# A hybrid attention layer: how the projections of the next head pair are dealt among the attention blocks of the current one

## The chip, the cores and the metric

The kernel runs on one core of a Trainium2 chip. The metric is the device time of one execution in microseconds. Three runs of the kernel before took 1989.61, 1990.07 and 1990.54 us (median 1990.07). The profile is of one more execution, which took 1991.46 us and whose profiled span is 1989.6 us.

## The reference, cut to what matters

The reference is one encoder layer, applied to two sequences with the same weights: a prompt of 1024 tokens (R below) and a sample of 512 tokens (S). Width 1024, heads of 64.

```python
hn = rms_norm(x, g_attn)
qa, ka, va, qd, kd, vd = split(hn @ w_in, 6)          # 8 heads each
oa = neighbourhood_attention(qa, ka, va, rpb)          # 2-D window, learned bias
od = dilated_attention(qd, kd, vd, slopes)             # three dilated windows merged
x  = x + concat(rms_norm(oa), rms_norm(od)) @ w_out
x  = x + (silu(hn2 @ w_gate) * (hn2 @ w_up)) @ w_down  # hn2 = rms_norm(x)
y  = rms_norm(x)
```

All of it is float32. The kernel multiplies float32 numbers as a sum of three products of high and low parts, so every projection of 128 features by 512 tokens is 8 x 3 = 24 matmuls. Probabilities and values are multiplied as float16 high and low parts.

## The kernel before, in words

The work up to about 850 us is projections and attention. Heads are taken two at a time ("pairs"): 16 pairs, first eight of R, then eight of S, alternately of kind b (dilated, heads `qd kd vd`) and kind a (neighbourhood). They are numbered from 0 here, as in the code: 0, 2, 4, 6 are R b; 1, 3, 5, 7 are R a; 8, 10, 12, 14 are S b; 9, 11, 13, 15 are S a.

A pair needs its projections: values, queries and keys, in this order (`ORDER`), each for every chunk of 512 tokens (two in R, one in S). That is 144 matmuls for an R pair and 72 for an S pair, all of line 155 (`mm3`, tile `acc`). A chunk's result is read out of its PSUM bank by `v_put`, `q_put` or `k_put`: ACT makes copies (high parts), DVE subtracts them from the bank (low parts). There are two such banks.

Then the pair's attention runs in blocks of 128 queries, 16 blocks in an R pair and 8 in an S pair: all blocks of its first head (`k.i` is 0), then all of its second (`k.i` is 1). `k.j` counts the blocks within a head, `k.st.nq` is their number. A block is on PE the scores (tile `sc`, lines 701 and 702), on DVE their sum with a bias table and the row's minimum (line 742), on ACT the exponentials (tile `t`, line 752), on PE the transposes of those (tile `pt`, line 763), on ACT the high part (line 769) and on DVE the low part (line 773) of the transposed, and for two blocks at a time on PE the product with the values (tile `pv`, line 785).

`step` writes the blocks out as a software pipeline. One step has the transposes of the block before, the softmax of this one, the value product of an earlier two, the scores of the next one, and then projections of a later pair from a generator, `dense`: `advance` draws one portion and `spent` counts the portions; `target` says how many portions are to be spent after a block. A portion is six matmuls, so an R pair's projections are 24 portions, an S pair's 12 (`totals`). `LEAD` shifts the target by so many blocks. Before the first scores of a new pair, `step` draws portions until that pair's keys are marked complete (`whole`).

Work that must come some portions later is put on an `agenda` by `after(n, ...)`; every portion drawn calls `tick`, which counts down. A chunk is read out two portions after its last matmul; low parts follow one portion later.

In most pairs PE, ACT and DVE execute in the order in which this code writes instructions (`manual_schedule`, the variable `core`). The exceptions are the blocks during which the projections of pair 4, of pair 7 and of pair 15, and after them the first output tiles, are dealt (`loose`): there a scheduling layer of the program orders the engines. These are, up to a few blocks at either end, the attention blocks of pairs 3, 6, 14 and 15.

Of the kernel before, what the change touches and what calls it, by code (L numbers as in the profile page):

```python
# [31 lines left out]
EPS = 1e-6  # L32
BW = 1600
LAG = 3
LEAD = 2
SQ = 4
TL = 3
NO = 4
# [18 lines left out]
def hymba_layer_kernel(  # L57
# [92 lines left out]
    def mm3(out, ops, first=True):  # L150

        i, last = 0, 3 * len(ops) - 1
        for (ah, al, bh, bl) in ops:
            for a, b in ((ah, bh), (ah, bl), (al, bh)):
                latest[0] = nc.tensor.matmul(out=out, lhsT=a, rhs=b, start=first and i == 0, stop=i == last,  # L155
                                              skip_group_check=not first)
                i += 1
                if i % 6 == 0:
                    yield

    agenda = []

    def after(n, fn):
        agenda.append([n, fn])

    def tick():
        for e in list(agenda):
            e[0] -= 1
            if e[0] <= 0:
                agenda.remove(e)  # L170
                e[1]()
# [3 lines left out]
            agenda.pop(0)[1]()  # L175

    def run(gen):
        for _ in gen:
            tick()

    order = [("b", 0), ("a", 0), ("b", 1), ("a", 1), ("b", 2), ("a", 2), ("b", 3), ("a", 3)]
    pairs = [(st, g, c) for st in (R, S) for g, c in order]
# [188 lines left out]
    def qkv(pi):  # L371
# [7 lines left out]
        def proj(which, ch):  # L379
            u = base + ORDER.index(which)  # L380
            w_split(u)
            wh, wl = ready[u]
            if u + 1 < n_in:
                w_load(u + 1)
            hh, hl = hT[st.name, ch]
            if which == 0:
                hh, hl = (z.rearrange("p k (q n c) -> p k n q c", q=8, n=4) for z in (hh, hl))
            acc = bank("tp" if pi == 0 and which == 1 else "mm", "acc")
            for i, _ in enumerate(mm3(acc, [(wh[:, k, :], wl[:, k, :], hh[:, k], hl[:, k]) for k in range(NK)])):
                if i == 1 and ch == st.nch - 1:  # L390
                    if u + 1 < n_in:
                        w_split(u + 1)
                    if u + 2 < n_in:
                        w_load(u + 2)
                if i == 3:
                    if pi:
                        after(2, lambda: (q_put, k_put, v_put)[which](ch, acc))
                    else:
                        (q_put, k_put, v_put)[which](ch, acc)
                yield  # L400

        def dst(z, ch):
            if g == "a":
# [92 lines left out]
        def k_put(ch, acc):  # L496
            if ch == 0:
                if st is S:
                    z = rb.tile([P, 2, T], F32R, tag="ka", name="ka", bufs=3)
                    res["k"] = [z[:, i] for i in range(2)]  # L500
                else:
                    res["k"] = [rb.tile([P, nx], F32R, tag="ka", name=f"ka{i}", bufs=3) for i in range(2)]
                res["kl"] = [klow[i][:, :nx] for i in (0, 1 + pi % 2)]
            ka, kl = res["k"], res["kl"]
            for n in range(2):
                for i in range(2):
                    nc.scalar.activation(dst(ka[i], ch)[own[i - n]], rev(acc[own[i]]), AF.Copy)

            def low(i):
                nc.vector.tensor_tensor(out=dst(kl[i], ch)[own[i]], in0=rev(acc[own[i]]),  # L510
                                        in1=dst(ka[i], ch)[own[i]].bitcast(F32), op=ALU.subtract)
                if ch == st.nch - 1 and nx > T:
                    borders(ka[i])
                    borders(kl[i], own[i])

            def lows():
                low(0)
                low(1)
                if ch == st.nch - 1:
                    res["whole"] = True  # L520

            after(1 if pi else 2, lows)

# [22 lines left out]

        done[pi] = res
        if pi == 0:
            rest = opening(proj)
            for _ in rest:  # L550
                yield
            return
# [13 lines left out]
        if by_chunk:  # L566
            turns.sort(key=lambda z: z[1])
        for which, ch in turns:
            for _ in proj(which, ch):
                next(extra, None)  # L570
                yield
        for _ in extra:
            yield

# [315 lines left out]
        yield  # L890

    def out_tile(i, ahead):
        for j, _ in enumerate(out_mm(i, st_out["wo"])):
            if j == 0:
                out_norm(i + 1)
            if j == 2 and i + 2 < ahead:
                out_pre(i + 2)
            if j == 5:
                out_tr(i + 1)
            yield  # L900

    def out_first():
        yield from out_start()
# [10 lines left out]
    def stream():  # L914
        for pi in range(1, len(pairs)):
            at[0] = pi
            for _ in qkv(pi):
                yield
        at[0] = len(pairs)
        yield from out_first()  # L920

# [2 lines left out]

    def advance(n=1):
        for _ in range(n):
            if next(dense, "end") == "end":
                return
            tick()
            spent[0] += 1  # L930

    def target(pi, j):

# [11 lines left out]
    def step(g):  # L945
# [20 lines left out]
            scores(todo[g + 1])  # L966
        if g + TL < len(todo):
            tables(todo[g + TL])
        while spent[0] < target(k.pi, k.j):
            was = spent[0]  # L970
            advance()
            if spent[0] == was:
                break
# [11 lines left out]
    while g < len(todo):  # L985
        with ExitStack() as fixed:
# [3 lines left out]
            while g < len(todo) and (at[0] in loose) == now:  # L990
                step(g)
                g += 1
    for _ in dense:
        tick()
    flush()
    while owed:
        head_out(owed.pop())
# [505 lines left out]
```

## Time and profile before

| | |
|---|---|
| median of 3 runs | 1990.07 us |
| profiled execution, its span | 1991.46 us, 1989.6 us |
| PE busy, share of the span | 1843.8 us, 93% |
| DVE busy | 1320.6 us, 66% |
| ACT busy | 915.6 us, 46% |
| POOL busy | 843.3 us, 42% |
| mean granted clock of TensorE | 0.973 |

The page divides the span in 40 slices of about 50 us; the first 17 or so are projections and attention, the rest the output projection and the feed-forward part. PE is the matmul engine, PEld its weight loads, which run beside matmuls. A matmul's shown duration is longer than the time to the next one's start, since they are pipelined; how fast PE goes is read from starts. Where PE has nothing to do, the timeline shows in brackets how long and what ended it.

The pairs stand in the trace one after the other. In the windows below a pair begins with the first score matmul of its first block and ends with that of the next pair's.

### The profile page before, as it was taken

The page shows a single profiled execution, that of the slowest core. Times are in us where ns is not written, and L with a number is a line of the kernel's source. Part 1 is how long each engine was busy: PE and PEld are TensorE (multiplying, and loading weights), DVE is VectorE, ACT ScalarE, POOL GpSimd, SP SyncE. Part 2 cuts the span into 40 slices and gives each one's busy share as a digit, 9 for nine tenths or more (in the row PEclk, how much of TensorE's full clock was granted, in tenths as well). Part 3 has the DMA queues.
Part 4 walks back from the last instruction along what each step waited for, and adds up shares of the span by engine and source line. Part 5 has one row for each costly group of instructions (what it writes and reads, how often), then busy time and mean ns, then how long its engine had stood idle before and what let it go on. Part 6 is the DMA issues. An engine that isn't in the chain of part 4 may idle for free.

```text
span 1989.6 us, 28959 instructions
## 1 busy us (share of the span) xinstructions
PE 1843.8 (93%) x10450; PEld 1619.5 (81%) x10450; DVE 1320.6 (66%) x2626; ACT 915.6 (46%) x1731; POOL 843.3 (42%) x691
## 2 busy tenths in 40 slices
PE   5899999989889998999899999989999997999998
PEld 4677777777677776878799999989999995887886
DVE  6565657755665556667877877787677764756765
ACT  4364566655566666444433334344333332423431
POOL 3223342233245543200466766766666652652120
PEclk9898999999999999999999999989999998999999
DMA  9333243332344445444334434433434438866652
GB/s 264 110 81 88 65 111 80 78 96 59 84 95 115 114 125 172 134 144 157 106 114 129 141 101 130 116 86 118 131 113 119 120 119 317 276 222 224 216 182 93
DMA packets 218943, 265.97 MB, mean 134 GB/s; under 512 B 59584, under 2 KB 163152, under 8 KB 218800
## 3 DMA queue, kind: packets, MB, share of 16 engines
q1 hardware_dynamic: 196176, 179.57, 29.7%
q0 software_dynamic: 22624, 84.56, 14.4%
q8 instruction: 82, 1.34, 0.3%
q14 instruction: 61, 0.50, 0.1%
HBM read 202.71 MB, written 51.41 MB: 128 GB/s over the span
## 4 chain that ended last, share of the span: by engine, by line
PE 47%; DMA 5%; DVE 4%; issue 3%; POOL 2%; ACT 1%; SPq 0%; DVEq 0%; POOLq 0%; ACTq 0%
PE acc L155 16%; PE yacc L155 13%; PE zacc L155 8%; PE mmacc L155 8%; DMA wq<-in_w_down_dram 2%; DMA left<-hid_d 1%; POOL wq L1284 1%; DVE flo L1126 1%; PE pt L210 1%; DMA hid_d<-as 1%; DMA wo_raw<-in_w_out_dram 0%; DVE left L1301 0%; ACT left L1300 0%; DVE dlo L1274 0%; POOL as L1244 0%
## 5 line engine op out<-in xcount | busy, mean ns | idle before, releaser
L155 PE MATMUL acc<-dhi,left 128*128 128x512 f32 x924 | 290.2, 395 | 15.4 <-ACT left L1300 13.6
L155 PE MATMUL acc<-hth,whi 128*128 128x512 f32 x576 | 236.3, 410 | 10.1 <-ACT hth L290 7.6
L155 PE MATMUL acc<-htl,whi 128*128 128x512 f32 x576 | 233.3, 405 | 6.8 <-POOL htl L293 3.7
L155 PE MATMUL acc<-hth,wlo 128*128 128x512 f32 x576 | 233.0, 405 | 0.9 <-POOL wlo L125 0.6
L1126 DVE TENSOR_TENSOR flo<-fs,fhi 128x512 fp32r<-128x512 f32 x176 | 174.8, 996 | 76.4 <-ACT fhi L1125 72.3
L773 DVE SCALAR_TENSOR_TENSOR pT<-pt,pT 128x512 f16<-128x512 f32 (+2 forms) x256 | 136.8, 553 | 132.5 <-ACT pT L769 130.9
L155 PEld LDWEIGHTS acc<-dhi,left 128*128 128x128 f32 x924 | 174.5, 189 | 56.1 <-ACT left L1300 14.4
L125 POOL TENSOR_TENSOR wlo<-wraw,whi 128x1024 fp32r<-128x1024 f32 x48 | 114.5, 2388 | 197.5 <-ACT whi L124 197.5
L1125 ACT ACTIVATE fhi<-fs 128x512 fp32r<-128x512 f32 x176 | 109.5, 628 | 183.4 <-POOL fs L1130 60.1
L769 ACT ACTIVATE pT<-pt 128x512 f16<-128x512 f32 (+2 forms) x256 | 118.9, 489 | 162.6 <-PE pt L763 159.3
L155 PE MATMUL acc<-dlo,left 128*128 128x512 f32 x462 | 181.8, 394 | 0.0
L1130 POOL TENSOR_TENSOR fs<-fraw 128x512 f32<-128x512 f32 x88 | 130.3, 1497 | 80.0 <-DMA fraw<-in_w_up_dram 70.0
L763 PE MATMUL pt<-ident,t 128*128 128x128 f32 x768 | 122.8, 282 | 44.2 <-ACT t L752 39.7
L1126 DVE TENSOR_TENSOR flo<-fraw,fhi 128x512 fp32r<-128x512 f32 x132 | 162.1, 1228 | 0.6 <-ACT fhi L1125 0.4
L1284 POOL TENSOR_TENSOR wq<-wq 128x512 f32<-128x512 f32 x55 | 93.2, 1706 | 157.9 <-DMA wq<-in_w_down_dram 128.2
L763 PEld LDWEIGHTS pt<-ident,t 128*128 128x128 f32 x768 | 89.8, 143 | 76.6 <-ACT t L752 56.9
L752 ACT ACTIVATE t<-t,mt 128x768 f32<-128x768 f32 (+3 forms) x192 | 137.9, 718 | 25.8 <-DVE mt L742 23.3
L1125 ACT ACTIVATE fhi<-fraw 128x512 fp32r<-128x512 f32 x132 | 83.0, 629 | 122.2 <-PE yacc L155 95.3
L155 PEld LDWEIGHTS acc<-hth,whi 128*128 128x128 f32 x576 | 111.8, 194 | 33.1 <-ACT hth L290 8.7
L155 PEld LDWEIGHTS acc<-htl,whi 128*128 128x128 f32 x576 | 112.1, 195 | 30.1 <-DVE htl L293 4.5
L155 PEld LDWEIGHTS acc<-hth,wlo 128*128 128x128 f32 x576 | 111.6, 194 | 28.7 <-POOL wlo L125 3.6
L1301 DVE TENSOR_TENSOR left<-left,left 128x1408 fp32r<-128x1408 f32 x42 | 74.4, 1774 | 81.6 <-ACT left L1300 81.5
(219 smaller groups left out, 4863.8 us busy)
## 6 DMA issues: line engine op xcount, KB each, us to landing
wq<-in_w_down_dram SPq DMA_DIRECT2D x132, 256.0 KB
hid_d<-as POOLq DMA_DIRECT2D x22, 1344.0 KB, 8.1
left<-hid_d SPq DMA_DIRECT2D x42, 704.0 KB
wraw<-in_w_in_dram POOLq DMA_DIRECT2D x46, 512.0 KB, 4.8
fraw<-in_w_gate_dram SPq DMA_DIRECT2D x45, 512.0 KB
fraw<-in_w_up_dram SPq DMA_DIRECT2D x45, 512.0 KB
tabb<-in_tabb_dram POOLq DMA_DIRECT2D x8, 800.0 KB, 5.6
xh<-x_d SPq DMA_DIRECT2D x12, 512.0 KB
```

The costliest lines, as they stand in the source:

```text
L125: eng.tensor_tensor(out=lo, in0=src, in1=hi.bitcast(F32), op=ALU.subtract))
L155: latest[0] = nc.tensor.matmul(out=out, lhsT=a, rhs=b, start=first and i == 0, stop=i == last, skip_group_check=not first)
L210: nc.tensor.transpose(out=pts[k // 4][:, k % 4 * P:(k % 4 + 1) * P], in_=src[:, k * P:(k + 1) * P], identity=ident)
L752: nc.scalar.activation(k.t, k.t, AF.Exp, bias=k.mt, scale=-1.0, accum_out=k.den)
L763: nc.tensor.transpose(out=pt[:, c * P:(c + 1) * P], in_=k.t[:, (c0 + c) * P:(c0 + c + 1) * P], identity=ident)
L769: nc.scalar.activation(hi, pt, AF.Copy, scale=16384.0)
L773: nc.vector.scalar_tensor_tensor(out=lo, in0=pt, scalar=16384.0, in1=hi, op0=ALU.mult, op1=ALU.subtract)
L1125: nc.scalar.activation(hi, src, AF.Copy)
L1126: nc.vector.tensor_tensor(out=lo, in0=src, in1=hi.bitcast(F32), op=ALU.subtract)
L1130: nc.gpsimd.tensor_tensor(out=o, in0=a, in1=b, op=op)
L1284: nc.gpsimd.tensor_tensor(out=src, in0=src, in1=other, op=q[1])
L1301: nc.vector.tensor_tensor(out=lo, in0=raw_lo, in1=hi.bitcast(F32), op=ALU.subtract)
```

## The change

Four things are changed.

`target` is called with the block's number in the pair, `k.i * k.st.nq + k.j`, where it was called with its number in the head, `k.j`.

`mm3` hands over after three matmuls instead of six. The first of two hand-overs is marked False; it draws no `tick`, and `spent` counts each as half a portion. So the agenda counts in the same six matmuls as before.

`LEAD` is 3 instead of 2.

`k_put` makes the first two of a key chunk's four ACT copies (those that the low parts are subtracted from) when it is called, and the other two one portion later, right before the low parts. The border columns of a b pair's keys in R are copied after both low parts and one portion later, and keys are marked complete one portion later as well.

```diff
-LEAD = 2
+LEAD = 3
...
-                if i % 6 == 0:
-                    yield
+                if i % 3 == 0:
+                    yield i % 6 == 0
...
     def run(gen):
-        for _ in gen:
-            tick()
+        for whole in gen:
+            if whole is not False:
+                tick()
...
-            for i, _ in enumerate(mm3(acc, [(wh[:, k, :], wl[:, k, :], hh[:, k], hl[:, k]) for k in range(NK)])):
+            i = -1
+            for whole in mm3(acc, [(wh[:, k, :], wl[:, k, :], hh[:, k], hl[:, k]) for k in range(NK)]):
+                if not whole:
+                    yield False
+                    continue
+                i += 1
...
-            for n in range(2):
+            def copy(n):
                 for i in range(2):
                     nc.scalar.activation(dst(ka[i], ch)[own[i - n]], rev(acc[own[i]]), AF.Copy)
 
+            copy(0)
+
             def low(i):
                 nc.vector.tensor_tensor(out=dst(kl[i], ch)[own[i]], in0=rev(acc[own[i]]),
                                         in1=dst(ka[i], ch)[own[i]].bitcast(F32), op=ALU.subtract)
-                if ch == st.nch - 1 and nx > T:
-                    borders(ka[i])
-                    borders(kl[i], own[i])
-
             def lows():
-                low(0)
-                low(1)
+                copy(1)
+                for i in range(2):
+                    low(i)
                 if ch == st.nch - 1:
-                    res["whole"] = True
+                    if nx > T:
+                        after(1, lambda: [borders(*z) for i in range(2) for z in ((kl[i], own[i]), (ka[i],))])
+                    after(1, lambda: res.update(whole=True))
...
-            if next(dense, "end") == "end":
+            whole = next(dense, "end")
+            if whole == "end":
                 return
-            tick()
-            spent[0] += 1
+            if whole is not False:
+                tick()
+            spent[0] += 1 if whole is None else 0.5
...
-        while spent[0] < target(k.pi, k.j):
+        while spent[0] < target(k.pi, k.i * k.st.nq + k.j):
```

Counted on PE between the first scores of one block and those of the next, the projection matmuls stand like this (pair 4 is like pairs 1, 2 and 5; pair 8 like 9 to 12):

| pair, its blocks | before | now |
|---|---|---|
| 0 (16) | 60 30 6 12 6 12 6 12 6 0 0 0 0 0 0 66 | 56 36, then 9 in each of 14 |
| 4 (16) | 0 18 6 12 6 12 6 12 6 0 0 0 0 0 0 66 | 9 in each |
| 6 (16, loose) | 12 20 2 16 1 9 0 0 20 3 1 0 24 0 24 12 | 9 9 10 8 9 9 0 0 24 0 51 3 0 0 0 12 |
| 7 (16) | 0 6 0 6 6 6 0 6 6 0 0 0 0 0 0 36 | 0 0, then 6 and 3 in turn in 12, 9 9 |
| 8 (8) | 0 18 6 12 6 0 0 30 | 9 in each |
| 13 (8) | 0 18 6 12 6 0 0 42 | 9 9 9 9 9 9 2 22 |

Pair 2 has 155 before and 148 now, pair 3 (loose) 133 and 140.

PE in the second head of pair 5 (R a), two blocks' scores (`sc`), transposes (`pt`) and the value product after them (`pv`); before:

```order
L701 MATMUL sc_4818<-ka1_4336,qa1_3890 128x384
L702 MATMUL sc_4818<-kl2_94,qa1_3890 128x384
L763 MATMUL pt_4826<-ident_69,t_4799 128x128 x3
L701 MATMUL sc_4839<-ka1_4336,qa1_3890 128x384
L702 MATMUL sc_4839<-kl2_94,qa1_3890 128x384
L763 MATMUL pt_4843<-ident_69,t_4830 128x128 x3
```

PE at the same blocks of pair 5, with a projection (`acc`) of pair 6; now:

```order
L709 MATMUL sc_4864<-ka1_4130,qa1_3860 128x384
L710 MATMUL sc_4864<-kl2_94,qa1_3860 128x384
L155 MATMUL acc_4829<-hth_104,whi_4674 128x512
L155 MATMUL acc_4829<-htl_105,whi_4674 128x512
L155 MATMUL acc_4829<-hth_104,wlo_4675 128x512
L155 MATMUL acc_4829<-hth_104,whi_4674 128x512
L155 MATMUL acc_4829<-htl_105,whi_4674 128x512
L155 MATMUL acc_4829<-hth_104,wlo_4675 128x512
L155 MATMUL acc_4829<-hth_104,whi_4674 128x512
L155 MATMUL acc_4829<-htl_105,whi_4674 128x512
L155 MATMUL acc_4829<-hth_104,wlo_4675 128x512
L771 MATMUL pt_4891<-ident_69,t_4845 128x128 x3
```

Three times the three products of a projection (high by high, low by high, high by low) now stand between a block's scores and the transposes of the block before it, where nothing stood.

DVE at the end of pair 1 (R a), when pair 2's keys become complete: low parts of keys (`kl0`, `kl1`, lines 510 and 518), borders (lines 413, 414, 419 and 420) and the scores' sums (`t,mt`, lines 742 and 750); before:

```order
L510 TENSOR_TENSOR kl0_92<-acc_1953,ka0_1960 64x512
L413 COPY ka0_1960<-ka0_1960 128x128
L414 COPY ka0_1960<-ka0_1960 128x128
L413 COPY kl0_92<-kl0_92 64x128
L414 COPY kl0_92<-kl0_92 64x128
L510 TENSOR_TENSOR kl1_93<-acc_1953,ka1_1961 64x512
L413 COPY ka1_1961<-ka1_1961 128x128
L414 COPY ka1_1961<-ka1_1961 128x128
L413 COPY kl1_93<-kl1_93 64x128
L414 COPY kl1_93<-kl1_93 64x128
L742 ISA t_2030,mt_2031<-sc_2019,tabb_1872 128x512
L742 ISA mt_2031 128x1
```

DVE at the same place; now:

```order
L518 TENSOR_TENSOR kl0_92<-acc_1832,ka0_1839 64x512
L518 TENSOR_TENSOR kl1_93<-acc_1832,ka1_1840 64x512
L419 COPY kl0_92<-kl0_92 64x128
L420 COPY kl0_92<-kl0_92 64x128
L419 COPY ka0_1839<-ka0_1839 128x128
L420 COPY ka0_1839<-ka0_1839 128x128
L419 COPY kl1_93<-kl1_93 64x128
L420 COPY kl1_93<-kl1_93 64x128
L419 COPY ka1_1840<-ka1_1840 128x128
L420 COPY ka1_1840<-ka1_1840 128x128
L750 ISA t_2006,mt_2007<-sc_1977,taba1_99 128x384
L750 ISA mt_2007 128x1
```

Both low parts come first and the borders after them, and a sum over a block of pair 1 (table `taba`) still follows them; before, the next sum was pair 2's first (table `tabb`).

## Rows read from the trace of the kernel before

**Rows 1.** Page, parts 1 and 2: busy time by engine; 40 slices
```profile
PE 1843.8 (93%) x10450; PEld 1619.5 (81%) x10450; DVE 1320.6 (66%) x2626; ACT 915.6 (46%) x1731; POOL 843.3 (42%) x691
...
PE   5899999989889998999899999989999997999998
...
PEclk9898999999999999999999999989999998999999
```

**Rows 2.** Windows by pair: length; busy (x instructions) PE, PEld, DVE, ACT, POOL; PEclk; DMA
```profile
86.40:148.20 61.80, 57.67 (x438) 48.92 (x437) 42.23 (x111) 39.96 (x81) 17.25 (x17) 1.00 0.27 69
148.20:208.50 60.30, 55.77 (x338) 45.61 (x338) 29.28 (x80) 30.34 (x68) 20.30 (x21) 0.92 0.29 79
208.50:282.60 74.10, 68.89 (x515) 58.15 (x514) 50.44 (x138) 45.23 (x92) 24.30 (x25) 1.00 0.31 80
328.70:401.20 72.50, 67.42 (x518) 57.12 (x517) 49.67 (x134) 45.61 (x95) 24.30 (x28) 1.00 0.29 74
401.20:459.00 57.80, 52.83 (x353) 43.04 (x352) 31.62 (x88) 31.90 (x70) 22.61 (x23) 1.00 0.30 82
459.00:531.60 72.60, 67.24 (x422) 53.50 (x421) 49.11 (x127) 41.40 (x80) 21.12 (x23) 0.95 0.30 78
531.60:548.80 17.20, 11.04 (x100) 9.00 (x98) 11.31 (x24) 7.80 (x17) 4.26 (x7) 0.91 0.31 95
548.80:585.10 36.30, 31.24 (x225) 25.00 (x223) 22.02 (x66) 22.94 (x56) 17.03 (x19) 1.00 0.47 103
641.40:671.10 29.70, 27.22 (x175) 21.75 (x174) 16.38 (x42) 18.87 (x39) 15.14 (x14) 1.00 0.45 104
671.10:697.40 26.30, 23.96 (x152) 19.62 (x150) 13.98 (x43) 15.37 (x38) 14.06 (x12) 1.00 0.48 119
727.10:758.80 31.70, 27.44 (x173) 22.15 (x171) 16.42 (x47) 16.07 (x39) 13.79 (x13) 1.00 0.47 127
```

**Rows 3.** Windows of two blocks without projections, and of a slow clock
```profile
115.19:120.37 5.18, 4.16 (x45) 3.63 (x45) 4.52 (x15) 3.57 (x8) 0.75 (x2) 1.00 0.36 119
568.59:572.15 3.56, 2.37 (x22) 1.71 (x22) 2.40 (x8) 2.17 (x6) 2.08 (x3) 1.00 0.35 95
183.80:194.10 10.30, 8.98 (x47) 7.33 (x48) 4.71 (x15) 4.42 (x13) 2.79 (x4) 0.50 0.28 89
```

**Rows 4.** Timeline of PE: one transpose of a block without projections, and its wait
```profile
115.19 0.88 PE L763 MATMUL pt<-ident,t 128*128 128x128 f32 x6 [1.01 <-ACT t L752]
```

**Rows 5.** Windows of two blocks with 18 projection matmuls; last row: four blocks
```profile
353.76:361.85 8.09, 8.09 (x63) 6.93 (x62) 6.68 (x18) 6.57 (x13) 2.07 (x3) 1.00 0.26 52
160.55:166.78 6.23, 6.23 (x41) 5.23 (x40) 3.70 (x11) 2.66 (x7) 1.40 (x2) 1.00 0.46 132
594.02:600.80 6.78, 6.78 (x48) 5.66 (x47) 4.33 (x14) 4.62 (x11) 6.51 (x7) 1.00 0.29 78
623.74:629.29 5.55, 5.55 (x35) 4.60 (x34) 3.21 (x12) 3.39 (x9) 4.50 (x5) 1.00 0.32 72
229.10:245.30 16.20, 15.85 (x123) 13.41 (x121) 13.86 (x37) 10.65 (x22) 5.91 (x6) 1.00 0.32 68
```

**Rows 6.** Timeline of PE: two successive projection matmuls in a long run
```profile
207.82 0.40 PE L155 MATMUL acc<-hth,whi 128*128 128x512 f32 x1
208.05 0.39 PE L155 MATMUL acc<-htl,whi 128*128 128x512 f32 x1
```

**Rows 7.** Waits, 75 to 900 us: total, times, longest
```profile
PE pt L763 <- ACT t L752: 39.7, 53, 1.2
...
PE sc L702 <- DVE kl L510: 3.6, 7, 1.6
...
DVE kl L510 <- ACT ka L507: 64.5, 22, 5.3
```

**Rows 8.** Lines of DVE in the third pair: low part of a key, border copy
```profile
L510 DVE TENSOR_TENSOR kl<-acc,ka 64x512 fp32r<-64x512 f32 x6 | 4.1, 688 | 10.3 <-ACT ka L507 10.2
...
L413 DVE CAST ka<-ka 128x128 fp32r<-128x128 f32 x2 | 0.4, 217 | 0.0
```

More of the change, by code (lines that the diff above doesn't have):

```diff
@@ L399, in proj @@
                         (q_put, k_put, v_put)[which](ch, acc)
-                yield
+                yield True
         def dst(z, ch):
@@ L548, in qkv @@
         if pi == 0:
-            rest = opening(proj)
+            rest = opening(lambda *a: (w for w in proj(*a) if w is not False))
             for _ in rest:
@@ L568, in qkv @@
         for which, ch in turns:
-            for _ in proj(which, ch):
-                next(extra, None)
-                yield
+            for whole in proj(which, ch):
+                if whole is not False:
+                    next(extra, None)
+                yield whole
         for _ in extra:
@@ L892, in out_tile @@
     def out_tile(i, ahead):
-        for j, _ in enumerate(out_mm(i, st_out["wo"])):
+        j = -1
+        for whole in out_mm(i, st_out["wo"]):
+            if whole is False:
+                yield False
+                continue
+            j += 1
             if j == 0:
@@ L899, in out_tile @@
                 out_tr(i + 1)
-            yield
+            yield True
     def out_first():
@@ L916, in stream @@
             at[0] = pi
-            for _ in qkv(pi):
-                yield
+            yield from qkv(pi)
         at[0] = len(pairs)
@@ L926, in advance @@
         for _ in range(n):
-            if next(dense, "end") == "end":
+            whole = next(dense, "end")
+            if whole == "end":
                 return
-            tick()
-            spent[0] += 1
+            if whole is not False:
+                tick()
+            spent[0] += 1 if whole is None else 0.5
     def target(pi, j):
@@ L992, in hymba_layer_kernel @@
                 g += 1
-    for _ in dense:
-        tick()
+    run(dense)
     flush()
```

## The prediction

> **What bounds the kernel now.** I read the page first, then windows cut at the pairs' borders, then PE's timeline inside a few pairs, then the waits. The page says that PE is busy 93% of the span; in its slices PE stands at 8 or 9 tenths where attention runs (the first 17) and at 9 later [rows 1]. So the room that a new order of projections can use is what PE stands still in the first 850 us.
>
> The windows by pair show where. A middle R b pair lasts 72.5 to 74.1 us with PE busy 67 to 69, an R a pair 57.8 or 60.3 with 53 to 56, an S b pair 29.7 with 27.2, an S a pair 26.3 with 24.0 [rows 2]. Busy PE flatters, since a matmul's modelled end reaches past the next one's start; a cleaner reading is by blocks. The old code gives every second head no projections, since its count starts again at 0 there, and what is left over comes in one run of 66 (S: 30) before the next pair. In the blocks without projections two R b blocks take 5.18 us of which PE is busy 4.16, two R a blocks 3.56 with 2.37 [rows 3]. The transposes stand and wait for the exponentials, 1.01 us in the row shown [rows 4]; from 75 to 900 us this wait adds up to 39.7 us in 53 places, and is PE's longest [rows 7].
>
> In the blocks of the first head with 6 and 12 projection matmuls by turns, that is 18 for two blocks, PE has no gap: two R b blocks take 8.09 us with PE busy 8.09, two R a blocks 6.23 of 6.23, two S b blocks 6.78 of 6.78, two S a blocks 5.55 of 5.55 [rows 5]. There PE is the bound.
>
> **The change part by part.** *The count that runs through the pair, with three matmuls at a time and LEAD 3.* Nine matmuls after each block are the same 18 for two blocks that the trace already shows, so the dealt rows give the new length of a pair without a model. What goes are the waits of the blocks without projections, and with them the run of 66; its matmuls fill the gaps. I take each pair by its window and its blocks:
>
> - pair 0: its last 14 blocks, 61.8 us [rows 2] with 126 matmuls, become 7 x 8.09 = 56.6: -5.2. The two before them get two matmuls more. A matmul costs 0.23 us from start to start [rows 6], 0.235 as I take it beside attention: +0.5.
> - pair 1: 60.3 becomes 8 x 6.23 = 49.8: -10.5. In it is a stretch of 10.3 us at half the clock, 0.50 granted, that began in blocks without projections [rows 3].
> - pair 2: 74.1 becomes 8 x 8.09 = 64.7, plus 4 matmuls over 144, 0.9: -8.5. The 7 that it no longer does come in pair 3: +1.6.
> - pair 4: 72.5 becomes 64.7: -7.8. Pair 5: 57.8 becomes 49.8: -8.0.
> - pair 6, ordered by the scheduling layer: the same 144 matmuls in another mixture, 72.6 us [rows 2]. I take 0.
> - pair 7 has only 72. Its first two blocks take 17.2 us [rows 2] with PE busy 11.0: a backlog from pair 6, which I keep; six matmuls leave it: -1.4. The next 12 get 9 for two blocks: PE's 2.37 us [rows 3] + 9 x 0.235 = 4.5, over the 3.56 that the chain needs, so 6 x 4.5 = 27.0; the last two are 6.23. 33.2 against 36.3 [rows 2]: -3.1.
> - pairs 8, 10 and 12, which the old order treats alike: 4 x 6.78 = 27.1 against 29.7: -2.6 each, -7.8. Pairs 9 and 11: 4 x 5.55 = 22.2 against 26.3 [rows 2, 5]: -4.1 each, -8.2.
> - pair 13: six blocks at 5.55 for two, 16.7; the last two have 24 matmuls, 5.55 + 6 x 0.235 = 7.0. 23.7 against 31.7 [rows 2], and 6 matmuls go to pair 14, +1.4: -6.6.
> - pairs 14 and 15 and the first output tiles are ordered by the scheduling layer; 0. What follows them stands in the order it had.
>
> Sum: -5.2 + 0.5 - 10.5 - 8.5 + 1.6 - 7.8 - 8.0 - 1.4 - 3.1 - 7.8 - 8.2 - 6.6 = -65.0 us.
>
> *The keys.* The work is the same: four copies, two subtractions of 688 ns for a chunk, eight border copies of 0.22 us for a b pair [rows 8]. What moves is where DVE stands. In the old order DVE waited 64.5 us for ACT's copies before it could subtract, 22 times [rows 7], with all later softmaxes behind it; but PE then had its run of 66, which hid this. Without that run the wait would be bare, and splitting the copies takes it away: the two copies that the subtraction reads are a portion old. I value this at nothing beside the dealt rows, since these rows hold no keys and it only makes the keys as light as queries, which they do hold: the two low parts of a chunk are 1.4 us for either.
>
> *Completion a portion later.* With LEAD 3, 27 portions of the 24 + 3 needed are spent before the last step of an R pair, so no run is needed before the first scores. But these scores stand right behind nine projections, the last block's transposes and a value product, and DVE has two low parts and, for b pairs, the borders to do in that time, 1.4 + 1.7 us. So a wait that the dealt rows don't have comes at the border of each of 13 pairs. From both sides: nothing, if DVE is early, or 1.6 us, the longest of seven waits of scores for a key's low part that the trace has, 3.6 us together [rows 7]. I take their mean, 0.5: 13 x 0.5 = +6.5, with +21 as the far end.
>
> -65.0 + 6.5 = -58.5. From the profiled execution, 1991.46 us for a span of 1989.6, this gives 1933.0; it stood 1.4 us over the median of the runs, so the median to expect is 1990.07 - 58.5 = 1931.6, say 1932.
>
> The scheduled stretches (pairs 3, 6, the start of 7, 14, 15) have no row that bounds their new mixture. The nearest: if the backlog at the start of pair 7 goes, its two blocks cost 3.6 us like others without projections: -12; if pair 6 loses what PE stands there, 72.6 less 67.2 [rows 2], -5. If a backlog like that one comes a second time, 17.2 - 3.6 = +14. I take 0, as the mixtures are alike.
>
> **A rule against it.** In a pair without a gap all granted clocks are 1.00 [rows 5], and the slow stretch stood among blocks with waits [rows 3]. The Trainium skill, "TensorE: Matmul & The Clock Gate", section "Loop structure matters more than you think", wants an output tile's matmuls back to back, with the next tile's following at once, and the change cuts such runs into nines. By that rule the clock could fall more often; the trace doesn't bear this out, as its dealt blocks are cut into sixes and twelves at full clock.
>
> **Rivals.** *The backlog dissolves* as well: 1932 - 12 - 5 and no wait at the borders, -6.5: 1908. For it: nine a block is gentler on DVE than a run. Against: rows of the sample's preparation still fall into pair 6.
>
> *Half the gain is lost* at the borders and in the scheduled stretches: waits at the far end, +14, and one more backlog, +14: 1960. For it: the order of three mixtures is not settled by this trace. Against: it needs both.
>
> *Slower: DVE runs late in every block.* In dealt blocks DVE is busy 13.86 of 16.2 us [rows 5], the highest of any stretch here, and keys and borders now stand between softmaxes. If DVE's slips make PE wait 1.0 us for each two blocks, as the exponentials do in the blocks without projections [rows 4], an R b pair takes 8 x 9.09 = 72.7, as much as now. There are 7 + 8 x 4 + 7 + 24 = 70 such twos: +70 - 58.5 = +11.5, 2002 us. It decides from 58.5 / 70 = 0.8 us on. Against: those same dealt rows have values and queries between softmaxes and PE never waits. The Trainium skill, same page, section "Architectural detail: the array is 16× 32×32, not 1× 128×128", calls VectorE's queue a strict FIFO; the waits of DVE on the copies of keys agree, and this is what such a slip would feed on.
>
> *No change*: the clock falls once in each of 12 pairs as it did in pair 1, at 10.3 us x 0.5 = 5.1 us: +61 - 58.5, 1993, or some other loss of the same size in all pairs. Only its price has a row [rows 3]; against it stand the clocks of [rows 5].
>
> **How the numbers follow.** The forecast has 0.64, within 1915 to 1949 by the bounds of the border waits (-6.5, +14) and small shifts of the scheduled pairs. The dissolved backlog has 0.13, half the gain 0.15, slower 0.05, no change 0.03. The range is 1905 to 1964. A measurement here tells 0.2%, some 4 us, from no change: faster 0.92, same 0.03, slower 0.05.
>
> **What would show it.** PE's timeline in pairs 1, 2, 4, 5: two blocks each 8.1 or 6.2 us through both heads, no run of 66 and no wait of transposes for exponentials; that wait's total down from 39.7 us to under 10, what is left lying in the scheduled pairs. Windows: an R b pair near 65 us, R a near 50, S b near 27.5, S a near 22.5. DVE's wait for key copies near 0. New waits of scores for key low parts or borders at pair borders, 0.5 us each. From the end of attention on, equal lengths. I am wrong if two dealt blocks take over 8.5 us with PE waiting for DVE, or if pairs 6 and 7 together move by more than 15 us.

## The result

The changed kernel takes 1957.41 us (median of 4 runs, 1954.25 to 1959.69); the kernel before took 1990.3 us beside it. The ratio is 0.9822, 95% interval 0.9805 to 0.9839: some 33 us less, where 58.5 were forecast. The direction was right and the time lies inside the range, but 25 us of the expected gain are missing, and the experiments below are about these.

### The profile page after: what moved, and what is told of

It is laid out like the page before. It is cut to its first block, busy times and chain, and to the rows that moved or that the text cites. A ratio compares the mean times of both kernels' runs of the same rounds, so it can differ in the third digit from the quotient of the medians.

```text
span 1953.8 us, 28948 instructions
## 1 busy us (share of the span) xinstructions
PE 1831.3 (94%) x10450; PEld 1616.0 (83%) x10450; DVE 1327.1 (68%) x2626; ACT 911.1 (47%) x1731; POOL 839.7 (43%) x691
## 4 chain that ended last, share of the span: by engine, by line
PE 72%; DVE 7%; DMA 6%; ACT 5%; issue 4%; POOL 2%; SPq 0%; DVEq 0%; ACTq 0%; POOLq 0%
PE acc L155 32%; PE yacc L155 13%; PE mmacc L155 9%; PE zacc L155 8%; PE pt L771 3%; DMA wq<-in_w_down_dram 2%; PE pv L793 2%; PE sc L709 2%; PE sc L710 2%; ACT t L760 1%; POOL wq L1297 1%; ACT ka L513 1%; DVE flo L1139 1%; DVE kl L518 1%; DMA hid_d<-as 1%
## 5 line engine op out<-in xcount | busy, mean ns | idle before, releaser
L1139 DVE TENSOR_TENSOR flo<-fs,fhi 128x512 fp32r<-128x512 f32 x176 | 168.4, 960 | 87.2 <-ACT fhi L1138 85.0
L155 PEld LDWEIGHTS acc<-dhi,left 128*128 128x128 f32 x924 | 174.3, 189 | 54.5 <-ACT left L1313 14.1
L1139 DVE TENSOR_TENSOR flo<-fraw,fhi 128x512 fp32r<-128x512 f32 x132 | 164.6, 1247 | 1.1 <-ACT fhi L1138 1.1
L808 POOL TENSOR_TENSOR ob<-ob,den 128x256 f32<-128x256 f32 x48 | 30.1, 628 | 254.9 <-DVE den L805 103.5
L155 PEld LDWEIGHTS acc<-htl,whi 128*128 128x128 f32 x576 | 111.5, 194 | 27.6 <-DVE htl L294 4.7
L1314 DVE TENSOR_TENSOR left<-left,left 128x1408 fp32r<-128x1408 f32 x42 | 75.9, 1809 | 79.2 <-ACT left L1313 79.2
```

The source lines that it names most:

```text
L1139: nc.vector.tensor_tensor(out=lo, in0=src, in1=hi.bitcast(F32), op=ALU.subtract)
L1314: nc.vector.tensor_tensor(out=lo, in0=raw_lo, in1=hi.bitcast(F32), op=ALU.subtract)
```

## The profile after

The profiled execution took 1955.61 us, its span is 1953.8 us, the mean granted clock 0.975. First the page: busy time by engine, and two lines of its 40 slices.

```profile
PE 1831.3 (94%) x10450; PEld 1616.0 (83%) x10450; DVE 1327.1 (68%) x2626; ACT 911.1 (47%) x1731; POOL 839.7 (43%) x691
...
PE   5899999988999999999999999889999997999998
...
PEclk9899999999999999999999999989999998999999
```

The work is the same (10450 matmuls, 2626 instructions of DVE as in [rows 1]); PE's slices are a little fuller where attention runs. The windows by pair answer to [rows 2], with the same columns: pairs 0 to 9, then pair 13, and from the first output tile to the end.

```profile
51.50:146.50 95.00, 86.49 (x545) 70.93 (x544) 56.84 (x143) 49.04 (x95) 23.93 (x24) 0.93 0.31 86
146.50:201.30 54.80, 52.30 (x342) 43.75 (x340) 32.55 (x82) 29.97 (x68) 20.96 (x22) 0.97 0.38 97
201.30:268.50 67.20, 64.19 (x475) 53.81 (x473) 45.83 (x129) 43.62 (x88) 27.20 (x27) 1.00 0.30 76
268.50:321.30 52.80, 51.81 (x353) 42.26 (x351) 33.45 (x99) 33.64 (x83) 16.84 (x24) 1.00 0.50 123
321.30:388.40 67.10, 64.12 (x486) 54.16 (x484) 47.34 (x130) 41.76 (x86) 20.23 (x21) 1.00 0.26 66
388.40:446.80 58.40, 52.26 (x335) 42.98 (x331) 37.41 (x95) 31.28 (x68) 24.64 (x25) 0.97 0.42 96
446.80:524.40 77.60, 69.68 (x506) 56.62 (x502) 58.47 (x140) 47.77 (x95) 21.53 (x28) 0.98 0.30 77
524.40:567.60 43.20, 37.58 (x268) 31.04 (x266) 25.22 (x70) 25.01 (x60) 20.42 (x22) 0.92 0.45 106
567.60:595.30 27.70, 27.14 (x186) 22.55 (x183) 16.36 (x42) 18.88 (x40) 15.84 (x15) 1.00 0.41 108
595.30:619.70 24.40, 23.28 (x155) 19.19 (x151) 14.19 (x42) 15.04 (x37) 14.12 (x14) 1.00 0.56 138
...
699.20:725.90 26.70, 24.75 (x156) 20.03 (x152) 15.76 (x45) 16.16 (x39) 16.45 (x16) 1.00 0.73 170
...
904.60:1953.80 1049.20, 999.22 (x5179) 931.53 (x5177) 739.90 (x1007) 385.50 (x626) 529.42 (x368) 0.98 0.47 151
```

The R b pairs 2 and 4 went from 74.1 and 72.5 to 67.2 and 67.1 us, not to 65.6 and 64.7; R a pair 1 to 54.8 and not 49.8; pair 5 did not gain at all, 58.4 against 57.8. From the first output tile on little changed (1049.2 us; before 1989.6 - 942.9 = 1046.7).

Windows of two blocks, in answer to [rows 5]: a dealt two in pair 4 and in pair 1, and the two slowest of pair 4.

```profile
329.25:337.24 7.99, 7.99 (x67) 6.90 (x65) 4.98 (x15) 4.57 (x12) 5.37 (x6) 1.00 0.27 82
153.62:159.74 6.12, 6.12 (x45) 5.21 (x43) 2.37 (x8) 2.16 (x7) 4.67 (x5) 1.00 0.41 131
361.64:371.32 9.68, 8.45 (x70) 7.04 (x67) 8.45 (x23) 5.84 (x14) 2.09 (x3) 1.00 0.35 56
371.32:380.57 9.25, 8.19 (x68) 6.81 (x65) 5.96 (x16) 5.82 (x12) 3.29 (x2) 1.00 0.25 70
```

So two dealt blocks without such a place are as the forecast took them, 8.0 and 6.1 us, PE busy throughout; a few fixed places are slower, and PE stands still there. In each of the two slowest it waits once for a softmax of DVE; the first of these waits:

```profile
363.59 0.39 PE L709 MATMUL sc<-ka,qa 128*128 128x256 f32 x1 [1.23 <-DVE mt L750]
```

The waits from 75 to 900 us say who waits for whom (total, times, longest):

```profile
DVE kl L518 <- ACT ka L513: 36.0, 18, 4.8
...
PE sc L709 <- DVE mt L750: 11.0, 10, 2.0
...
DVE qa L549 <- ACT qa L545: 10.8, 8, 2.5
...
PE pt L771 <- ACT t L760: 7.0, 11, 1.7
...
PE acc L155 <- DVE qa L549: 4.1, 2, 2.0
PE sc L710 <- DVE kl L518: 3.9, 7, 0.9
```

The wait of the transposes for the exponentials, 39.7 us in [rows 7], is down to 7.0. In its place PE waits for DVE: for softmaxes (`mt`), low parts of queries and of keys. And DVE still waits 36.0 us for the copies of keys, which the forecast had near 0.

**First place: the keys.** ACT, DVE and PE at the border of pair 7 and pair 8. The four copies of line 513 are shown as two pairs; the second ends at 567.86.

```profile
562.28 1.19 ACT L513 ACTIVATE ka<-acc 64x512 fp32r<-64x512 f32 x2
...
565.58 1.05 ACT L124 ACTIVATE whi<-wraw 128x1024 fp32r<-128x1024 f32 x1
566.65 1.21 ACT L513 ACTIVATE ka<-acc 64x512 fp32r<-64x512 f32 x2
```

```profile
567.89 1.41 DVE L518 TENSOR_TENSOR kl<-acc,ka 64x512 fp32r<-64x512 f32 x2 [2.22 <-ACT ka L513]
```

```profile
568.62 0.50 PE L710 MATMUL sc<-kl,qa 128*128 128x512 f32 x1 [0.56 <-DVE kl L518]
```

The two copies that the subtraction reads ended at 563.47. It begins 4.4 us later, 0.03 us after the other two, which stand behind a weight split of 1.05 us on ACT. Those other two write other partitions of the same tiles. The same 0.03 us stands at all four such places from 185 to 270 us.

**Second place: the values' borders.** GpSimd and DVE in pair 5, then what PE waited for, and the clock after it.

```profile
412.57 1.49 POOL L812 DMA_DIRECT2D o_ap<-ob  x2 [0.29 <-POOL ob L808]
414.08 2.39 POOL L125 TENSOR_TENSOR wlo<-wraw,whi 128x1024 fp32r<-128x1024 f32 x1
```

```profile
413.28 3.25 DVE L419 COPY v<-v 128x128 f16<-128x128 f16 x1
416.45 0.18 DVE L420 COPY v<-v 128x128 f16<-128x128 f16 x1
...
416.87 1.39 DVE L549 SCALAR_TENSOR_TENSOR qa<-acc,qa 64x512 fp32r<-64x512 f32 x2
```

```profile
418.40 0.47 PE L155 MATMUL acc<-hth,whi 128*128 128x512 f32 x1 [2.04 <-DVE qa L549]
```

```profile
418.80:422.20 3.40, 3.37 (x11) 2.45 (x10) 1.33 (x6) 2.20 (x6) 0.00 (x0) 0.50 1.24 131
```

The first of four equal copies takes 3.25 us, the others 0.18. It ends at 416.53, just after GpSimd's `tensor_tensor` (416.47). The low parts of the queries stand behind it, PE waits 2.04 us for the bank they read, and then runs 3.4 us at a granted clock of 0.50, which is 1.2 of 2.4 GHz. Pair 1 shows the same: a copy from 171.34 to 174.59, the `tensor_tensor` until 174.52, a wait of 2.04 us at 176.46.

## The experiments

Ratios are to the kernel before, run beside each batch (1993.1, 1992.2 and 1989.2 us in three batches), with 95% intervals. The theory from the profile, called A: the running count brings the gain, and what is missing is lost at fixed places where a queue's head waits. The rivals are told with each run. The first four take the change apart.

**e1_count**: the kernel before with the running count alone.

```diff
-        while spent[0] < target(k.pi, k.j):
+        while spent[0] < target(k.pi, k.i * k.st.nq + k.j):
```

> The kernel before with one edit: the target's block number runs through the pair. LEAD 2, six matmuls at a time and the old keys stay. Theory A (the running count brings the gain, what falls short of the forecast is PE waiting at fixed places for a DVE that stands behind an ACT copy or behind POOL): 1955 to 1965 us, PE's waits of transposes for exponentials under 12 us in total. Theory B (the count is worth the forecast 58 us, and LEAD 3, threes and the keys' delay give back half of it): 1945 us or less.

1951.31 us, ratio 0.9789 (0.9764 to 0.9813): no worse than the whole change and between the bands of the two theories, so the other parts together gained nothing beside it. Its window of pair 5 shows no loss, that of pair 6 a large one:

```profile
377.00:425.40 48.40, 47.34 (x319) 40.21 (x316) 29.82 (x85) 28.15 (x63) 18.64 (x18) 1.00 0.34 94
425.40:517.40 92.00, 80.11 (x515) 64.34 (x514) 60.07 (x152) 51.12 (x101) 28.37 (x35) 0.89 0.29 77
```

**e2_keys**: the kernel before with the key part alone (the `k_put` of the diff).

> The kernel before with the keys' part alone: copies in two halves, borders and completion a portion later. Theory A: within 5 us of the kernel before, since the run before each pair hides both orders. Theory B: 6 us or more slower, since each of 13 runs gets six matmuls longer and new scores wait for borders.

1989.46 us, ratio 0.9973 (0.9956 to 0.9991): next to nothing. DVE's waits for key copies did not go, they are 75.7 us in 18 places against 64.5 in 22.

**e3_no_keys**: the changed kernel with the old `k_put`.

> The changed kernel with the old keys' part. Theory A: within 6 us of the changed kernel (1957): DVE waits as long or longer for ACT's key copies (36 us in the changed kernel from 75 to 860 us), PE's waits for scores' banks behind it stay at about 1.1 us twice in each R b pair. Theory B: 6 us or more faster, since keys are complete a portion earlier.

1939.35 us, ratio 0.9733 (0.9712 to 0.9754): 18 us less than the change. Beside the other parts the key part costs time: A, which had the two within 6 us of each other, is wrong here, and B's number holds; B's reason, the earlier completion of keys, falls with e10. DVE's waits for key copies are 5.6 us in 5 places.

**e4_lead2**: the changed kernel with the old lead.

```diff
-LEAD = 3
+LEAD = 2
```

> The changed kernel with LEAD 2. Nine more matmuls then stand before each new pair's first scores and none after them. Theory A: 0 to 8 us slower than the changed kernel (one block without projections in each pair, some 0.5 us of PE each), waits of scores for keys nearly gone. Theory B: 6 us or more faster.

1971.98 us, ratio 0.9899 (0.9878 to 0.992): 14.6 us more. Pairs 5 and 6 take 63.4 and 85.1 us at clocks of 0.92 and 0.90, against 58.4 and 77.6 at 0.97 and 0.98. A had allowed 8 us; the lead is worth more.

The next four test the places themselves.

**e5_low_first**: the changed kernel, subtractions ahead of the second pair of copies.

```diff
             def lows():
-                copy(1)
                 for i in range(2):
                     low(i)
+                copy(1)
```

> The changed kernel with one line moved: in lows both subtractions stand before copy(1), instead of behind it. Theory A (the subtraction on VectorE waits for the second pair of key copies, which the change writes just before it, and those stand behind the exponentials in ScalarE's queue): the waits of DVE kl for ACT ka, 36.0 us in 18 places of the changed kernel, fall under 15 us; the 16 to 18 us that the key part costs there (1957.4 against 1939.35 without it) mostly come back: 1940 to 1948 us. Rival B (the key part costs its time by what it delays at the end of a projection, borders and the release of the keys a portion later, whatever the order of copies): the waits fall but the time stays at 1953 to 1960 us.

1951.5 us, ratio 0.9796 (0.9771 to 0.9821). DVE's waits for key copies fell from 36.0 to 7.7 us, and the subtraction in block 13 of pair 2 starts without a wait:

```profile
251.56 1.38 DVE L518 TENSOR_TENSOR kl<-acc,ka 64x512 fp32r<-64x512 f32 x2
```

In the changed kernel it started later, after 1.99 us for ACT:

```profile
254.50 1.39 DVE L518 TENSOR_TENSOR kl<-acc,ka 64x512 fp32r<-64x512 f32 x2 [1.99 <-ACT ka L513]
```

Pair 4 takes 64.9 us (67.1), pairs 8, 10 and 12 26.9, 26.6 and 26.6 (27.7, 27.6, 27.6). So the data did not make it wait, the place of the copies did. The median gained only 5.9 us, with intervals that overlap; between the bands of A and B, and where the rest went comes below.

**e6_vborder_act**: the changed kernel with the old `k_put`, the values' f16 border copies on ACT (`borders` takes the copying call as an argument).

```diff
                 if nx > T:
-                    borders(z)
+                    borders(z, copy=lambda out, in_: nc.scalar.activation(out, in_, AF.Copy))
```

> The changed kernel with the old key part (1939.35 us), and the two f16 border copies of the values moved from VectorE to ScalarE. Theory A (these copies take 3.25 us on VectorE where a GpSimd tensor_tensor runs beside them, and the low part of the queries stands behind them): the copies take under 0.5 us each, the 2.04 us waits of PE in pairs 1 and 5 and the half clock behind them go: 4 to 9 us under 1939.35, 1930 to 1935 us. Rival B (the end of the GpSimd work, or the accumulator's release, is late there anyway): copies short, but PE waits in the same places for something else, 1937 to 1943 us.

1928.25 us, ratio 0.9679 (0.9656 to 0.9702): 11 us under e3, a little more than A expected. Two of the copies, and the windows of pairs 1 and 5:

```profile
404.78 0.51 ACT L464 ACTIVATE v<-v 128x128 f16<-128x128 f16 x2
```

```profile
147.30:197.40 50.10, 50.10 (x343) 42.75 (x340) 28.84 (x78) 30.70 (x72) 20.99 (x22) 1.00 0.40 108
...
380.00:431.60 51.60, 49.68 (x334) 42.18 (x330) 33.63 (x85) 31.86 (x72) 24.68 (x25) 1.00 0.40 108
```

In e3 these two took 54.5 and 59.9 us at clocks of 0.97 and 0.94:

```profile
146.50:201.00 54.50, 52.09 (x342) 43.79 (x339) 32.38 (x84) 29.75 (x68) 20.97 (x22) 0.97 0.39 98
...
383.90:443.80 59.90, 53.36 (x333) 44.39 (x330) 38.82 (x90) 31.75 (x70) 26.20 (x25) 0.94 0.42 97
```

The forecast had 49.8 for each.

**e7_early_read**: the changed kernel with the old `k_put`, results read out one portion earlier, low parts one later.

```diff
-                        after(2, lambda: (q_put, k_put, v_put)[which](ch, acc))
+                        after(1, lambda: (q_put, k_put, v_put)[which](ch, acc))
...
-            after(1 if pi else 2, lows)
+            after(2, lows)
...
-            after(1 if pi else 2, low)
+            after(2, low)
```

> The changed kernel with the old key part (1939.35 us), the copies out of an accumulator one portion after its last matmul instead of two, the low parts two after the copies instead of one. Theory A (low parts wait for copies that are late in ScalarE's queue, and the softmax behind them makes PE wait 1.2 us once in each of the R b pairs): these waits go, 3 to 6 us under 1939.35, 1933 to 1936 us. Rival B (read a portion earlier, the copies stand at the head of ScalarE's queue and wait for PE there; exponentials behind them are late): PE waits for t of ACT grow from 7 us to over 15 us, 1941 to 1952 us.

1942.06 us, ratio 0.9743 (0.9718 to 0.9768): not faster than e3. Neither theory tells it all. The waits in the R b pairs went, as A said (pair 4: 63.4 us, PE busy 63.40), the value copies took 0.19 us each, as they no longer stood beside GpSimd's split, and PE's wait for exponentials that B expected to grow fell to 4.8 us. Up to pair 13 the profile is 11 us ahead of e3; all of that is lost behind it.

**e8_three**: e6 and e7 together, and the `dgs` tile taken from other buffers (`ra` tag `t` in place of `rb` tag `p16`).

> The changed kernel with the old key part (1939.35 us), with the edits of the two runs before (border copies of the values on ScalarE, copies a portion earlier and low parts two after them), and the dgs tile taken from the buffers of t instead of those of p16, which a DMA transpose reads. Theory A (three separate waits at fixed places): their gains add, 8 to 15 us under 1939.35, 1924 to 1931 us, and the wait of DVE dgs for the transposes (5.3 us in pair 5 of the changed kernel) goes. Rival B (the stretches drawn closer only move the wait to ScalarE's queue or to the pairs that the schedule sets): 1936 to 1945 us.

1939.8 us, ratio 0.9734 (0.971 to 0.9759): rival B. Again ahead up to pair 13 and slow behind it.

The last four ask whether the losses add, what the other half of the key part costs, what the threes bring, and whether a further border helps.

**e9_both**: the changed kernel, its key part kept, with the edits of e5 and e6.

> The changed kernel, its key part kept, with both repairs: the two subtractions ahead of copy(1), and the f16 border copies of the values on ScalarE. Theory A (two separate losses, 5.9 us and 11.1 us where each was repaired alone): they add, 1957.4 - 17 = 1940, 1936 to 1944 us. Rival B (the loss at the borders was large only because the keys were issued the old way, or the clock takes the gain back): 1946 to 1955 us.

1933.16 us, ratio 0.9717 (0.97 to 0.9735): 24 us less than the change. The two repairs add; alone they gave 5.9 and 11.1 us, and the 7 us beyond this sum lie within the intervals of the kernels compared.

**e10_delay**: e3 with borders and release of the keys one portion later, as in the change.

```diff
                 if ch == st.nch - 1:
-                    res["whole"] = True
+                    if nx > T:
+                        after(1, lambda: [borders(*z) for i in range(2) for z in ((kl[i], own[i]), (ka[i],))])
+                    after(1, lambda: res.update(whole=True))
```

> The changed kernel with the old key copies (all four, then the low parts a portion later: 1939.35 us), but with the other half of the key part: border copies and the release of the keys one portion later, low parts' borders ahead of the copies'. Theory A (what the key part costs beyond the order of copies, 1951.5 against 1939.35, is this delay): 1948 to 1953 us. Rival B (the delay costs nothing; the remaining 12 us of that comparison come from where the half-clock stretches and the projections near pairs 13 to 15 fall): 1936 to 1944 us.

1939.88 us, ratio 0.9747 (0.973 to 0.9763): the delay costs nothing. The splitting of the copies is all that is left between e10 and the change, so what the key part costs is there; e5, which keeps the splitting, gets back only a third of it.

**e11_sixes**: e6, projections dealt six at a time.

```diff
-                if i % 3 == 0:
-                    yield i % 6 == 0
+                if i % 6 == 0:
+                    yield True
...
-            spent[0] += 1 if whole is None else 0.5
+            spent[0] += 1
```

> The version with old keys and value borders on ScalarE (1928.25 us), with projections dealt six matmuls at a time as before the change instead of three; running count and LEAD 3 kept. Theory A (the threes take a wait from each block: a portion of six is 1.4 us, and the blocks alternate between one and two of them): 1936 to 1946 us. Rival B (the running count and the lead bring all of it, the size of a portion nothing): 1924 to 1933 us.

1937.25 us, ratio 0.9738 (0.9721 to 0.9755): 9 us more, as A expected. DVE's waits for key copies come back (27.4 us in 14 places against 5.5 in 5), and the S b pairs take 28.4, 28.4 and 28.1 us instead of 26.9, 26.5 and 26.6. The R pairs together are about as long as with threes (pairs 1 to 6: 362.9 us, 361.0 in e6). In the profiled executions only 1.7 us of the loss lie ahead of pair 13, the rest behind it.

**e12_borders**: e6 with the keys' f32 borders on ACT too.

```diff
                 if ch == st.nch - 1 and nx > T:
-                    borders(ka[i])
-                    borders(kl[i], own[i])
+                    act = lambda out, in_: nc.scalar.activation(out, in_, AF.Copy)
+                    for i in range(2):
+                        borders(ka[i], copy=act)
+                    for i in range(2):
+                        borders(kl[i], own[i], act)
```

> The version with old keys and value borders on ScalarE (1928.25 us), with the f32 border copies of the keys (ka, then kl) on ScalarE as well, behind both subtractions. Theory A (a border copy on VectorE beside a GpSimd tensor_tensor waits for its end wherever the two meet: a pair of kl copies took 3.59 us in pair 5): 1 to 4 us under 1928.25, 1924 to 1927 us. Rival B (ScalarE waits there for VectorE's subtraction with exponentials behind it): 1928 to 1934 us.

1928.1 us (1924.12 to 1937.44), ratio 0.9701 (0.9675 to 0.9727): the same as e6, at the lower end of B's band. Pair 5 falls from 51.6 to 49.9 us, pair 6 rises from 76.7 to 79.2. e6 is the version to take; it beats both kernels.

Where the differences lie is seen best with each profiled span cut at the first scores of pair 13. Up to there most pairs are ordered by hand; pairs 14 and 15 behind it are ordered by the scheduling layer.

| kernel | up to pair 13, us | from there on, us |
|---|---|---|
| before | 727.1 | 1262.5 |
| e2 keys alone | 721.3 | 1270.1 |
| change | 699.2 | 1254.6 |
| e1 count alone | 685.1 | 1263.5 |
| e4 lead 2 | 710.5 | 1259.6 |
| e3 old keys | 689.0 | 1247.3 |
| e10 old keys, delay | 688.5 | 1247.9 |
| e5 lows first | 692.4 | 1260.6 |
| e9 lows first, borders | 673.7 | 1261.0 |
| e6 old keys, borders | 677.2 | 1248.2 |
| e7 old keys, early | 677.9 | 1260.4 |
| e8 three edits | 676.5 | 1261.5 |
| e11 e6 with sixes | 678.9 | 1255.1 |
| e12 e6, more borders | 675.7 | 1246.6 |

Each row is one execution. Runs of one kernel can lie 13 us apart (e12), and the stretch ahead of pair 1 alone lasts 141.2 to 147.4 us in the kernels with the running count, so small differences between two rows need not come from the edit. The left column follows theory A: writing the lows first gives 6.8 us, moving the values' borders 11.8 with old keys (e6 less e3) and 18.7 with split ones (e9 less e5), of which 4.8 lie ahead of pair 1. The right column stands at some 1247 us with the old key copies, threes, LEAD 3 and late reading, and at 1255 to 1264 in the other kernels with the running count. Pair 13 to the first output tile holds part of it (202.7 us in e3, 210.7 in e5), the remaining work the rest (1044.6 and 1049.9). Which mixture of instructions there makes the difference, and how much of it is chance, was not tried; it stays open. It is about 7 of the 18 us between the change and e3.

## Why the prediction was right in sign and short in size

In the table, by groups of pairs, are the forecast's terms, the difference of the profiles, and that of e6, in which both places are repaired (all in us).

| | forecast | change | e6 |
|---|---|---|---|
| up to the end of pair 0 | -4.7 | -1.7 | -0.9 |
| R a pairs 1 and 5 | -18.5 | -4.9 | -16.4 |
| R b pairs 2 and 4 | -16.3 | -12.3 | -17.9 |
| pairs 3, 6, 7 | -2.9 | +1.4 | -2.0 |
| S b pairs 8, 10, 12 | -7.8 | -6.5 | -9.4 |
| S a pairs 9, 11 | -8.2 | -3.9 | -3.3 |
| pairs 13 to 15 | -6.6 | -10.4 | -10.0 |
| borders of 13 pairs | +6.5 | in the rows above | in the rows above |
| first output tile to the end | 0 | +2.5 | -4.3 |
| sum | -58.5 | -35.8 | -64.2 |

*The dealt rows held.* Two dealt blocks take 8.0 and 6.1 us where nothing else comes in, and in e6 the R pairs 1, 2, 4 and 5 gained 34.3 us where 34.8 were forecast. There, reading the new length of a pair from rows of the kernel before was sound. That the whole of e6 comes to -64 us beside the -65.0 of the count is in part luck: the S a pairs are 4.9 us short, and pairs 13 to 15 and what follows gained 7.7 more than forecast.

*The keys were valued at nothing; this step failed.* The forecast gave the key part no time because "splitting the copies takes it away: the two copies that the subtraction reads are a portion old". The data were old, but the subtraction waited for the two that were not: `copy(1)` is written just before it, on the same tiles. e5 shows it by moving one line. The key part costs 10.2 us up to pair 13 (699.2 less 689.0), 6.8 of them by this order; what it costs behind pair 13 is not explained. The remark that keys are only as light as queries missed this, since queries have no second pair of copies.

*A loss had no term at all.* In pairs 1 and 5 the new deal puts the values' border copies beside a weight split of GpSimd. Before, the six copies of that line from 75 us on took 0.19 us in the middle and 0.34 at most:

```profile
L413 DVE COPY v<-v x6: 187/194/335, 172.2 to 425.4; 128x128 f16<-128x128 f16 x6
```

The forecast counted only borders of keys. The loss is 11 us with old keys (e6 less e3) and 18 with split ones (e9 less e5). No rival named it; "half the gain is lost", which gave 1960, has the size but not the place. The Trainium skill, "SBUF — State Buffer", section "Who interferes with whom", says that VectorE copies in two-port modes and GpSimd share a pair of ports, and that the one that comes later is blocked for the whole instruction. The trace agrees as to the block (3.25 us against 0.18, ending 0.06 us after GpSimd's instruction); that these copies run in such a mode no row here shows. The copy is shown to begin 0.80 us ahead of that instruction, while GpSimd issued a DMA, so which of these held it is not settled. Elsewhere either one alone goes with a long copy. In the changed kernel the first of two border copies of keys, which take 0.22 us each at other places, begins inside a `tensor_tensor`:

```profile
446.33 2.39 POOL L125 TENSOR_TENSOR wlo<-wraw,whi 128x1024 fp32r<-128x1024 f32 x1 [0.89 <-ACT whi L124]
...
446.69 2.37 DVE L419 CAST kl<-kl 64x128 fp32r<-64x128 f32 x2
```

In the kernel before one such copy took 0.75 us: it began at 459.77, beside a DMA issue of GpSimd that ran from 459.55 to 460.48, and ended just after it. The forecast could have been warned by it.

*The clock.* In pair 1 of e6, where PE never waits, its clock is 1.00; where it waited 2.04 us in pairs 1 and 5, 3.4 us at half clock followed. The projections cut into nines did not lower it by themselves, as the forecast said.

*Borders and S pairs.* The first scores of a pair wait 0.3 to 0.9 us for key lows and borders, near the 0.5 that the forecast took. The S a pairs gained less: the first two blocks of pair 9 take 7.7 us in the change and 8.0 in e6 instead of 5.55. PE waits for 1.1 and 1.6 us of this; beside the waits, the last transposes and a value product of the S b pair before stand there. In e6 the wait has the same neighbour as the second place. DVE's low parts of the pair's values take 2.73 us beside a `tensor_tensor` of GpSimd and 0.87 without one, and the exponentials that PE waits for come behind them:

```profile
574.27 2.38 POOL L125 TENSOR_TENSOR wlo<-wraw,whi 128x1024 fp32r<-128x1024 f32 x1 [1.86 <-ACT whi L124]
...
574.60 2.73 DVE L481 SCALAR_TENSOR_TENSOR va<-vT,vsc,va 128x256 f16<-128x256 f32 x2
...
579.02 0.66 PE L770 MATMUL pt<-ident,t 128*128 128x128 f32 x4 [1.62 <-ACT t L759]
```

The same 2.7 us stand at the start of pairs 11 and 13, and in e3 and e9; no run moved these low parts. The S b pairs of e6 gain 1.6 us more than forecast, which makes up a part.

*Scheduled pairs.* Pairs 3, 6 and 7 moved by +6.7, +5.0 and -10.3 us: as a sum near the forecast, singly not.

*Signs of being wrong.* Of the two signs of being wrong, pairs 6 and 7 moving together by more than 15 us did not come true (-5.3). The other one did: in pair 4 two successive blocks took 9.7 us and the next two 9.3, over 8.5, with PE waiting for DVE. So the rival in which DVE runs late had the mechanism, but at a few places and not in every block.

*A reading.* The rival's remark that DVE's 13.86 of 16.2 us is the highest share of any stretch is wrong: two blocks without projections have 4.52 of 5.18 [rows 3]. Its price does not rest on it.

*Lead and threes* were counted only within the running count. e4 and e11 price them: 14.6 us for the lead (with the new keys), 9 us for the threes (with old keys and repaired borders). Beside the running count alone, with old keys, neither was tried by itself.

## What to carry to other kernels

Rows of a stretch that already runs in the planned mixture give a good price for the plan, but only for what stands in that stretch: list what else will be issued between those instructions (copies, borders, weight splits), and on which engine each will have a neighbour. An instruction that is split to shorten a wait helps only if the late half is written behind the one that waits. After such a change, read each engine's longest single instruction against its usual duration.

## What the hardware showed that was not expected

A DVE copy of 128x128 f16 took 3.25 us beside a GpSimd `tensor_tensor` of 2.39 us, and 0.18 without it. Two f32 copies of 64x128 in e6 did the same beside two such instructions, which ran from 420.49 to 425.20:

```profile
420.49 4.71 POOL L125 TENSOR_TENSOR wlo<-wraw,whi 128x1024 fp32r<-128x1024 f32 x2 [2.74 <-ACT whi L124]
```

```profile
420.80 0.56 DVE L749 CUSTOM_DVE_ANT_0 t<-sc,taba 128x384 f32<-128x384 f32 x1
...
421.70 3.59 DVE L420 CAST kl<-kl 64x128 fp32r<-64x128 f32 x2
```

The sum of scores and bias at 420.80, beside the same GpSimd instructions, took its usual 0.56 us.
